# The first two value chunks of an mLSTM layer: a quarter of the contraction in seven products instead of eight

## The chip, the cores and the metric

The kernel runs on one core of one Trainium2 chip. The time is device microseconds of one execution; the figure before is the median of three runs, 1020.14 us (1020.08 to 1020.18). One more execution was taken with the hardware profiler; all durations, starts and shares below are of that one.

Engines by their names in the profile: PE is TensorE (PEld its weight loads), DVE VectorE, ACT ScalarE, POOL GpSimd, SP SyncE.

## The reference, cut to what matters

A decoder trunk of two layers, model width 2048, 256 tokens, fp32. The second layer is an xLSTM mLSTM with 8 heads (width of keys 128, of values 256):

```python
u = hn @ o_w_in[j]
qk = u[..., 0:2 * C_QK]                       # 2048 columns: queries and keys
v = u[..., 2 * C_QK:2 * C_QK + C_WIDTH]       # 2048 columns: the values, four chunks of 512
...                                           # output gate, silu gate, input and forget gates
qk = jax.nn.silu(causal_conv(qk, c_conv_w[j], c_conv_b[j]))
yc = mlstm(q, k, v, li, lf)                   # needs q, k, v and the gates
yc = head_rmsnorm(yc, c_norm[j]) * jax.nn.sigmoid(og) * jax.nn.silu(z)
h = h + yc @ o_w_out[j]
```

## The kernel before

**Products.** Every projection is computed with the activations (128 contraction rows x 128 tokens) held in TensorE and 512 columns of weights streamed, into a 128x512 PSUM bank for each half of the tokens. A number is kept as a high and a low part, and one product of two such numbers is three matmuls: high by high, high by low, low by high. A chunk of 512 columns has a contraction of 2048: four quarters, each 4 x 128 rows, two halves of the tokens, three matmuls, so 24 matmuls a quarter and 96 a chunk (`quarter_tok`, L211 to L213; `product`, L235, where three lines are one).

**Weights.** They come from HBM as 128x1024 tiles of 512 KB, two to a quarter, issued by SyncE into a ring of five (`raw`). ScalarE casts a tile to its high part (`whi`, L137 or L221) and VectorE subtracts that to get the low part (`wlo`, L138 or L222), into rings of four. A tile can be cast only once TensorE has read the tile four places ahead of it.

**Seven products (`seven`).** For two chunks of columns at once, one quarter of the contraction (`kq` = 0) can be done as a 2x2 matrix product in seven instead of eight, by the well-known scheme of Strassen and Winograd: two halves of the tokens, two halves of the quarter, two chunks. Each of the products is six matmuls. It needs four sums of activations (`combos`, made beforehand, here for the quarter 0 by `early()`, kept in `qs`), and sums of weights: the tile X (first chunk, first half) becomes W = X + the second chunk's first half, then W + Y, then that plus Z; the tile Y becomes Y + the second chunk's first half. Sums of two loaded tiles are additions on VectorE (`add`, L310), or, with `acc`, a transfer issued by POOL that adds while it writes (`add_loaded`, L314), which can start once the tile has been split for its own use. The results lie in four banks A, F, B and E; ScalarE copies A into F and its negative into B (L345, L346), saves B twice to SBUF (`keep`, L322), and VectorE adds what is left with `soon` (L318). The other three quarters are plain (`plain`). The order of the pieces is the string `a5a6.2aA7b.4F.bb` (L26): a digit is a product, a and b are the plain quarters of the first and second chunk, a point is a pump, A and F hand out a bank.

**Order of the work.** Side work is written as generators, called lanes. `pump()` makes one step of every lane, behind the latest product, cast, split and load; it is called in each quarter after the first half of the tokens, and at the points. `drain(lane)` runs a lane to its end. A scheduler then orders each engine's instructions by priorities, and `high_priority` lifts weight splits (400) and the copies at the end of a chunk (450). An engine executes its own list in order; where an instruction waits, what stands behind it waits as well.

**Around the change.** The four chunks of queries and keys come first (`oqk`); each is written to HBM and read back transposed by POOL (`features`, L686 and L689), then goes through the causal convolution as three VectorE operations of some 254 columns for each of 16 pieces (L1218) and a multiplication (L1222). Then the four value chunks (`ov`). In them run the lanes of the features, of the gates (`gate_stats`, L1257 to L1285: 8x256 rows of scans and sums; it ends in `split_rows`, L424 to L426, which makes the tile s8 of the running maxima) and of the heads: `mix(c)` takes a pair of heads, called head c below (0 to 3). Its steps are the spread of a row of s8 over all partitions by TensorE (L431), decays on VectorE and ScalarE (L1305 to L1311), high and low parts of queries and keys (L1322, L1323), scores (L1329 to L1331), their high and low parts (L1334, L1335), and the sums over values (L1349). Values go from their bank to SBUF with a row factor (L1394, L1395). When the two halves of chunk 0 are out, `values` drains two feature lanes and starts the four heads' lanes.

Chunks 2 and 3 of the values are made by `seven`; chunks 0 and 1 by `project_tok`.

Of the kernel before, what the change touches and what calls it, by code (L numbers as in the profile page):

```python
# [11 lines left out]
F32 = mybir.dt.float32  # L12
# [7 lines left out]
P = 128  # L20
# [25 lines left out]
def trunk(ctx: ExitStack, tc: tile.TileContext, a, out):  # L46
# [22 lines left out]
    def step(lane):  # L69
        q = lanes.get(lane)  # L70
        while q:
            if next(q[0], lanes) is not lanes:
                return True
            q.pop(0)
        return False
# [8 lines left out]
    def drain(*which):  # L84
        for lane in which:
            while step(lane):
                pass
# [75 lines left out]
    def project_tok(w, j, act, before=None, begun=None):  # L163

        ps = begun or [pm.tile([P, 512], F32, name="mm", tag="mm") for _ in range(2)]
        for kq in range(1 if begun else 0, 4):
            if before is not None:
                before(kq)
            quarter_tok(w, j, kq, act, ps)
        return ps  # L170
# [16 lines left out]
    def two_and_seven(w, act, before, where, places, home=None, begin=None):  # L187

        qs = {}
        start("combos", combos(act, 0, qs, *where))  # L190
        for c, ps in enumerate(project_two(w, act, before)):
            for hf in range(2):
                yield c, hf, ps[hf]
        drain("combos")
        if begin is not None:
            begin()
        for b, hf, src in seven(w, 2, act, qs, (0,), *places(), home and home()):
            yield 2 + b, hf, src

    def quarter_tok(w, j, kq, act, ps):  # L200

        parts = load_weights(w[4 * j + kq])
        for hf in range(2):
            for kk in range(4):
                k = kq * 4 + kk
                hi, lo = parts[kk // 2]
                c = (kk % 2) * 512
                ah, al, _ = act[k // 2]
                xh, xl = (tokens(x, k % 2, hf) for x in (ah, al))
                wh, wl = hi[:, c:c + 512], lo[:, c:c + 512]  # L210
                te.matmul(ps[hf], xh, wh, start=(k == 0), stop=False, skip_group_check=True)  # L211
                te.matmul(ps[hf], xh, wl, start=False, stop=False, skip_group_check=True)  # L212
                last["pe"] = te.matmul(ps[hf], xl, wh, start=False, stop=(k == KT - 1), skip_group_check=True).ins  # L213
            if hf == 0:
                pump()
# [374 lines left out]
    def ready(act, lane):  # L590

        def before(kq):
            while 2 * kq + 1 not in act:
                step(f"{lane}{kq}")
        return before
# [14 lines left out]
    def ple_gate(hq, parts, pls, rp, hss, gain, lane, more):  # L610

        nxt = {}
        for c, hf, src in parts:
            drain("pg")
            th = tp.tile([P, 512], F32, name="th", tag="th")
            h = hq[c][:, hf]
            s.activation(th, src, AF.Tanh, scale=0.5)
            v.scalar_tensor_tensor(th, th, 1.0, pls[c][hf], op0=ALU.add, op1=ALU.mult)
            v.scalar_tensor_tensor(h, th, rp[:, hf:hf + 1], h, op0=ALU.mult, op1=ALU.add)
            if not hf:  # L620
                continue
            start(f"{lane}{c}", to_features(hq[c], c, nxt, gain, lane, more))
            step(f"{lane}{c}")
            for hf in range(2):
                squared(hq[c][:, hf], hss[:, c, hf:hf + 1])
        return nxt
# [14 lines left out]
    acth = []  # L641
# [133 lines left out]
    if True:  # L775
        ew = a["ew"]
        fs, qs, ks, xcs = {}, {}, {}, {}
# [313 lines left out]
        for g in range(2):  # L1091
            ps = project_tok(ew, 6 + g, acth)
# [33 lines left out]
    def pieces(tile):  # L1126
        return iter([tile[:, 0:512], tile[:, 512:1024]]).__next__
# [30 lines left out]
    acth = ple_gate(hq, two_and_seven(a["g0"], act, ready(act, "fe"), (e0, "q4", 2), in_e0), pls, rp0, hss0, "on", "fg", gate_sums)  # L1158
# [34 lines left out]
    with tc.tile_pool(name="m1", bufs=2) as m1:  # L1193
# [32 lines left out]
        qs = {}  # L1226
# [148 lines left out]
        turn = []  # L1375

        def value_halves():
            for j in range(2):
                for hf, ps in enumerate(project_tok(a["ov"], j, acth)):
                    yield j, hf, ps  # L1380
            drain("combos", "spill")
            store_of.extend(hp.tile([P, 1024], F32, name="pr", tag="h") for _ in range(2))
            for b, hf, src in seven(a["ov"], 2, acth, qs, (0,), chain, part, acc=True):
                yield 2 + b, hf, src

        def values():
            for j, hf, src in value_halves():
                if hf == 0:
                    vt = m1.tile([P, 2, 2, VW], F32R, name="vt", tag="vt", bufs=6)
                    gp.memset(vt.bitcast(F32)[:, :, :, 256:VW], 1.0)  # L1390
                    vl = ap.tile([P, 1024], F32R, name="vl", tag="ahl").rearrange("p (h i e) -> p h i e", h=2, i=2)
                with tc.high_priority(offset=450):
                    src = src.rearrange("p (i e) -> p i e", i=2)
                    s.activation(vt[:, hf, :, 0:256], src, AF.Copy, scale=norm["rt"][:, hf:hf + 1])  # L1394
                    v.scalar_tensor_tensor(vl[:, hf], src, norm["rt"][:, hf:hf + 1], vt[:, hf, :, 0:256].bitcast(F32),  # L1395
                                           op0=ALU.mult, op1=ALU.subtract)
                if hf == 0:
                    continue
                vts.append((vt, vl))
                if j == 0:  # L1400
                    drain("qk0", "qk2")
                    for c in range(4):
                        start("mix", mix(c))
                    start("mix", mix_norm())
# [36 lines left out]
        for jj in (0, 2):  # L1441
            us = [m1.tile([P, 2, 512], F32, name="u", tag="vt", bufs=6) for _ in range(2)]
            for b, hf, src in pair(a["oz"], jj, True):
                j, u = jj + b, us[b]
# [292 lines left out]
```

## Time and profile before

| | |
|---|---|
| median of three runs | 1020.14 us |
| the profiled execution | 1020.23 us |
| its span, first to last instruction | 1018.4 us |
| granted TensorE clock | 0.998 |
| TensorE busy | 1009.4 us, 99% |
| VectorE busy | 842.8 us, 83% |
| ScalarE busy | 661.4 us, 65% |
| POOL busy | 101.3 us, 10% |
| first product of value chunk 0 | starts at 561.38 us of the span |

Matmuls overlap in their pipe: a matmul's row lasts from its start to its modelled end, so a list of starts tells the pace, and the busy time of a group counts the overlap. Rows of the chain of waits end where the next begins. In a view by windows, the number in brackets behind a busy time is the count of instructions. Instructions of the same line and shape that follow each other are joined in one row, with their count behind an x.

### The profile page before, as it was taken

The numbers are of one execution on the slowest core, as the hardware profiler recorded it, in microseconds if no ns is written. First come the engines' busy times: TensorE is split into PE (matmuls) and PEld (weight loads), VectorE is DVE, ScalarE is ACT, GpSimd is POOL, SyncE is SP. The second block draws the span as 40 slices with busy tenths as digits, with TensorE's granted clock in tenths as the row PEclk, the third lists the DMA queues.
The fourth block names the chain that finished last, engine by engine and source line by source line (L and its number), as shares of the span: only waits on it lengthen the run. The fifth ranks groups of instructions, "written<-read, shape, count | busy, mean of one in ns | idle before, by whom it ended". The sixth has DMA issues, their size and how long they took to land.

```text
span 1018.4 us, 14515 instructions
## 1 busy us (share of the span) xinstructions
PE 1009.4 (99%) x5158; PEld 838.1 (82%) x5158; DVE 842.8 (83%) x1234; ACT 661.4 (65%) x949; POOL 101.3 (10%) x182
## 2 busy tenths in 40 slices
PE   9999999999999999999999999999999999999996
PEld 8888888888888888888888888888888888888886
DVE  7858969969687887898669997888889997999794
ACT  7675554686875554666557877776676777466562
POOL 0111101011111112021011100000011110102000
PEclk9999999999999999999999999999999999999999
DMA  9987756567778799487798757567879889696852
GB/s 364 330 233 240 225 177 197 166 204 225 251 235 305 238 315 291 155 284 249 258 337 250 228 166 227 166 208 201 256 193 283 233 249 356 181 288 217 279 186 83
DMA packets 69816, 242.66 MB, mean 238 GB/s; under 512 B 9040, under 2 KB 10448, under 8 KB 69744
## 3 DMA queue, kind: packets, MB, share of 16 engines
q1 hardware_dynamic: 56016, 198.08, 58.7%
q0 software_dynamic: 13296, 43.13, 16.1%
q8 instruction: 40, 0.66, 0.3%
q10 hardware_dynamic: 432, 0.52, 0.1%
q14 instruction: 32, 0.26, 0.1%
HBM read 221.78 MB, written 19.92 MB: 237 GB/s over the span
## 4 chain that ended last, share of the span: by engine, by line
PE 99%; ACT 0%; DMA 0%; issue 0%; DVE 0%; ACTq 0%; POOLq 0%
PE mm L235 29%; PE mm L211 14%; PE mm L212 14%; PE mm L213 14%; PE mx L235 8%; PE mx L211 3%; PE mx L212 3%; PE mx L213 3%; PE mm L517 1%; PE nu L1349 1%; PE mx L517 1%; PE mm L1562 1%; PE mm L1561 1%; PE mm L1563 1%; PE st L213 1%; PE st L235 1%
## 5 line engine op out<-in xcount | busy, mean ns | idle before, releaser
L137 ACT CAST whi<-raw 128x1024 fp32r<-128x1024 f32 (+1 forms) x309 | 322.6, 1047 | 211.3 <-PE mm L213 95.2
L138 DVE TENSOR_TENSOR wlo<-raw,whi 128x1024 fp32r<-128x1024 f32 (+1 forms) x309 | 371.6, 1213 | 104.0 <-ACT whi L137 97.8
L211 PE MATMUL mm<-whi,ahl 128*128 128x512 f32 x640 | 250.5, 392 | 0.0
L212 PE MATMUL mm<-wlo,ahl 128*128 128x512 f32 x640 | 249.4, 390 | 0.0
L213 PE MATMUL mm<-whi,ahl 128*128 128x512 f32 x640 | 249.3, 389 | 0.0
L235 PE MATMUL mm<-whi,ahl 128*128 128x512 f32 x720 | 231.8, 390 | 0.0
L235 PEld LDWEIGHTS mm<-whi,ahl 128*128 128x128 f32 x720 | 135.2, 188 | 27.9
L211 PEld LDWEIGHTS mm<-whi,ahl 128*128 128x128 f32 x640 | 120.2, 188 | 25.5 <-issue 0.4
L213 PEld LDWEIGHTS mm<-whi,ahl 128*128 128x128 f32 x640 | 120.2, 188 | 25.1
L235 PE MATMUL mm<-wlo,ahl 128*128 128x512 f32 x360 | 140.5, 390 | 0.0
L212 PEld LDWEIGHTS mm<-wlo,ahl 128*128 128x128 f32 x640 | 120.2, 188 | 24.3
L222 DVE TENSOR_TENSOR wlo<-ch,whi 128x1024 fp32r<-128x1024 f32 x67 | 81.1, 1221 | 12.5 <-ACT whi L221 11.1
L221 ACT CAST whi<-ch 128x1024 fp32r<-128x1024 f32 x67 | 70.1, 1050 | 26.8 <-PE mm L235 13.8
L235 PEld LDWEIGHTS mm<-wlo,ahl 128*128 128x128 f32 x360 | 67.6, 188 | 14.1 <-DVE wlo L222 0.3
L235 PE MATMUL mx<-whi,ahl 128*128 128x512 f32 x192 | 63.3, 390 | 0.0
L212 PE MATMUL mx<-wlo,ahl 128*128 128x512 f32 x128 | 49.8, 389 | 0.0
L213 PE MATMUL mx<-whi,ahl 128*128 128x512 f32 x128 | 49.8, 389 | 0.0
L211 PE MATMUL mx<-whi,ahl 128*128 128x512 f32 x128 | 49.8, 389 | 0.0
L235 PE MATMUL mm<-whi,q 128*128 128x512 f32 x144 | 49.1, 391 | 0.0
L235 PEld LDWEIGHTS mx<-whi,ahl 128*128 128x128 f32 x192 | 36.1, 188 | 7.9 <-ACT xr L575 0.4
L235 PE MATMUL mx<-wlo,ahl 128*128 128x512 f32 x96 | 37.4, 390 | 0.0
L235 PEld LDWEIGHTS mm<-whi,q 128*128 128x128 f32 x144 | 27.0, 188 | 5.7
(389 smaller groups left out, 1318.5 us busy)
## 6 DMA issues: line engine op xcount, KB each, us to landing
raw<-in_ew_dram SPq DMA_DIRECT2D x64, 512.0 KB, 5.2
raw<-in_g_dram SPq DMA_DIRECT2D x60, 512.0 KB, 4.5
raw<-in_oqk_dram SPq DMA_DIRECT2D x32, 512.0 KB, 5.5
raw<-in_eo_dram SPq DMA_DIRECT2D x30, 512.0 KB, 5.1
raw<-in_oo_dram SPq DMA_DIRECT2D x30, 512.0 KB, 6.4
raw<-in_ov_dram SPq DMA_DIRECT2D x29, 512.0 KB, 4.2
raw<-in_oog_dram SPq DMA_DIRECT2D x24, 512.0 KB, 4.1
raw<-in_oz_dram SPq DMA_DIRECT2D x20, 512.0 KB, 5.1
```

The source lines that it names most:

```text
L137: last["act"] = s.copy(h, r).ins
L138: last["dve"] = v.tensor_tensor(out=l, in0=r, in1=h.bitcast(F32), op=ALU.subtract).ins
L211: te.matmul(ps[hf], xh, wh, start=(k == 0), stop=False, skip_group_check=True)
L212: te.matmul(ps[hf], xh, wl, start=False, stop=False, skip_group_check=True)
L213: last["pe"] = te.matmul(ps[hf], xl, wh, start=False, stop=(k == KT - 1), skip_group_check=True).ins
L221: last["act"] = s.copy(hi, r).ins
L222: last["dve"] = v.tensor_tensor(out=lo, in0=r, in1=hi.bitcast(F32), op=ALU.subtract).ins
L235: last["pe"] = te.matmul(o, x, y, start=(first and k + i == 0), stop=(end and k == n - 1 and i == 2), skip_group_check=True).ins
L517: last["pe"] = te.matmul(ps[hf][:, o:o + w_], tokens(pact[x], k, hf), (hi, lo)[y][:, k * 512 + o:k * 512 + o + w_], start=(n == mine[0]), ...
L1349: te.matmul(ps[:, 0:n], x[:, i, o:o + P], y[:, b, i], start=(b == 0 and x is sh and y is vh), stop=(b == hf and y is vl))
L1561: te.matmul(o, xh, wh, start=(k == 0), stop=False)
L1562: te.matmul(o, xh, wl, start=False, stop=False)
```

## The change

Chunks 0 and 1 of the values are made by `seven` as chunks 2 and 3 are, with the first quarter of the contraction in seven products and two of the sums of weights by accumulating transfers (`acc=True`). The saved banks lie in a tile of the pool `m1` with the tag "vt". The lane of the sums of activations (`combos`) is drained ahead of this, and the lane `spill` behind the first two chunks, as before.

```diff
         def value_halves():
-            for j in range(2):
-                for hf, ps in enumerate(project_tok(a["ov"], j, acth)):
-                    yield j, hf, ps
-            drain("combos", "spill")
+            drain("combos")
+            pr = pieces(m1.tile([P, 1024], F32, name="pr", tag="vt", bufs=6))
+            yield from seven(a["ov"], 0, acth, qs, (0,), chain, pr, acc=True)
+            drain("spill")
             store_of.extend(hp.tile([P, 1024], F32, name="pr", tag="h") for _ in range(2))
             for b, hf, src in seven(a["ov"], 2, acth, qs, (0,), chain, part, acc=True):
                 yield 2 + b, hf, src
```

The order of the chunks' halves changes with it: both chunks are ready close together, at the end of 186 matmuls, where chunk 0 was ready after 96 and chunk 1 after 192. The heads' lanes start after chunk 0's second half, as they did.

TensorE's list where the first spread of a head stands, before (mm_5562 is a bank of value chunk 1, s8 the split maxima):

```order
L211 MATMUL mm_5562<-whi_5571,ahl_4392 128x512
L212 MATMUL mm_5562<-wlo_5572,ahl_4392 128x512
L213 MATMUL mm_5562<-whi_5571,ahl_4392 128x512
L431 MATMUL mx_5588<-s8_5445,identr_229 128x256 x2
L211 MATMUL mm_5563<-whi_5565,ahl_4386 128x512
L212 MATMUL mm_5563<-wlo_5566,ahl_4386 128x512
```

And with the change (mm_5351 is the bank B of the first seven products, mm_5779 the bank A of the second):

```order
L235 MATMUL mm_5351<-whi_5727,ahl_4810 128x512
L235 MATMUL mm_5351<-whi_5733,ahl_4816 128x512
L431 MATMUL mx_5680<-s8_5488,identr_229 128x256 x2
L235 MATMUL mm_5351<-wlo_5734,ahl_4816 128x512
L235 MATMUL mm_5351<-whi_5733,ahl_4816 128x512 x2
L235 MATMUL mm_5351<-wlo_5734,ahl_4816 128x512
L235 MATMUL mm_5351<-whi_5733,ahl_4816 128x512
L235 MATMUL mm_5779<-whi_5784,ahl_4386 128x512
```

The spread stood in the first quarter of chunk 1, behind 108 matmuls of the values; now it stands behind 181, five matmuls ahead of the end of both chunks.

VectorE's list ahead of the row L426 that completes s8, before:

```order
L425 CAST s8_5445<-Mx_5341 8x256
L1222 SCALAR_TENSOR_TENSOR qk_5414<-th_5496,qk_5414 128x512
L138 TENSOR_TENSOR wlo_5572<-raw_5570,whi_5571 128x1024
L1395 SCALAR_TENSOR_TENSOR vl_5557<-mm_5347,rcr_4629,vt_5555 128x512
L426 TENSOR_TENSOR s8_5445<-Mx_5341,s8_5445 8x256
L138 TENSOR_TENSOR wlo_5612<-raw_5610,whi_5611 128x1024
```

And with the change (ch_5782 and ch_5797 are the tiles X and Y of the second seven products, pr_5347 the saved bank of the first):

```order
L138 TENSOR_TENSOR wlo_5734<-raw_5732,whi_5733 128x1024
L1276 TENSOR_TENSOR ae_5342<-li_5337,Bc_5340 8x256
L1395 SCALAR_TENSOR_TENSOR vl_5588<-pr_5347,rcr_4629,vt_5586 128x512
L1278 TENSOR_TENSOR ae_5342<-Bc_5340,Mx_5341 8x256
L318 TENSOR_TENSOR pr_5347<-mx_5348,pr_5347 128x512
L425 CAST s8_5488<-Mx_5341 8x256
L1285 STREAM_TRANSPOSE aT_5343<-ae_5342 32x64
L426 TENSOR_TENSOR s8_5488<-Mx_5341,s8_5488 8x256
```

L426 stood behind a split of chunk 1's first quarter; now all weight splits of both chunks stand ahead of it, and the first two of chunks 2 and 3.

TensorE's list at the first scores, before (wlo_5719 and wlo_5725 belong to the last quarter of chunk 1):

```order
L213 MATMUL mm_5562<-whi_5724,ahl_4816 128x512
L1329 MATMUL mx_5741<-qhl_5699,khl_5700 128x256 x3
L1330 MATMUL mx_5741<-qk_5147,qk_5414 128x128
L1329 MATMUL mx_5747<-qhl_5699,khl_5700 128x256 x3
L1330 MATMUL mx_5747<-qk_5147,qk_5414 128x128
L211 MATMUL mm_5563<-whi_5718,ahl_4810 128x512
```

And with the change (mm_5779 and mm_5780 are banks of the second seven products):

```order
L1329 MATMUL mx_5833<-qhl_5750,khl_5751 128x256 x2
L235 MATMUL mm_5779<-wlo_5997,ahl_4816 128x512
L235 MATMUL mm_5779<-whi_5996,ahl_4816 128x512
L235 MATMUL mm_5780<-whi_5990,ahl_4810 128x512
L235 MATMUL mm_5780<-wlo_5991,ahl_4810 128x512
L1329 MATMUL mx_5833<-qhl_5750,khl_5751 128x256
L1330 MATMUL mx_5833<-qk_5147,qk_5457 128x128
```

The scores stood in one piece in chunk 1; now they stand in pieces in the second seven products.

## The prediction

> **What bounds the kernel now.** I read the page's busy shares and its chain first, then TensorE's waits.
>
> ```profile
> span 1018.4 us, 14515 instructions
> PE 1009.4 (99%) x5158; PEld 838.1 (82%) x5158; DVE 842.8 (83%) x1234; ACT 661.4 (65%) x949; POOL 101.3 (10%) x182
> PE 99%; ACT 0%; DMA 0%; issue 0%; DVE 0%; ACTq 0%; POOLq 0%
> PE st L99 <- PEq L1728: 0.8, 1, 0.8
> ```
>
> The chain that ended last is TensorE from end to end, and in the whole run it waits once, 0.8 us at the start. So the time is the number of matmuls by their pitch, and two things alone can move it: fewer products, or a first wait. The pitch comes from the list of starts and from the chain:
>
> ```profile
> 572.34 0.39 PE L211 MATMUL mm<-whi,ahl 128*128 128x512 f32 x1
> 572.57 0.39 PE L212 MATMUL mm<-wlo,ahl 128*128 128x512 f32 x1
> ...
> 672.09 14.77 PE mm L235 x65
> ```
>
> Starts lie 0.23 us apart, and 14.77/65 = 0.227 us, for the matmuls of the plain chunks and of the seven products alike (0.2266 used below). The 0.39 us of a row is its latency in the pipe. The windows show who could make TensorE wait (the change lies from 561 to 647):
>
> ```profile
> core 0: us, PE busy (x) PEld busy (x) DVE busy (x) ACT busy (x) POOL busy (x), PEclk, DMA share, GB/s
> 540.00:560.00 20.00, 20.00 (x90) 16.57 (x89) 20.00 (x34) 15.39 (x26) 2.92 (x7) 1.00 0.81 256
> 560.00:580.00 20.00, 20.00 (x91) 16.53 (x90) 18.63 (x34) 16.31 (x24) 2.75 (x5) 1.00 0.80 241
> 580.00:600.00 20.00, 20.00 (x90) 16.57 (x90) 19.66 (x37) 15.14 (x25) 0.00 (x0) 1.00 0.57 184
> 600.00:620.00 20.00, 20.00 (x103) 16.99 (x103) 16.66 (x24) 15.96 (x31) 2.01 (x4) 1.00 0.64 162
> 620.00:640.00 20.00, 20.00 (x105) 17.13 (x103) 15.71 (x23) 15.36 (x32) 0.00 (x0) 1.00 0.68 232
> 640.00:660.00 20.00, 20.00 (x107) 16.93 (x106) 15.87 (x24) 13.30 (x27) 0.00 (x0) 1.00 0.48 152
> ```
>
> VectorE is busy 58.3 of 60 us (97%) from 540 to 600, where the first two value chunks are made, and 79 to 83% in each stretch behind that. ScalarE is at 65 to 82%. TensorE's clock is full. A change that takes work from TensorE and gives it to VectorE just there is where a wait can arise.
>
> **What it removes.** The first quarter of the contraction for two chunks and two token halves is 8 products of six matmuls, and 7 now. So 6 x 0.2266 = **1.36 us** less on TensorE, 0.13% of the run. By the mean of a row it would be another sum:
>
> ```profile
> L235 PE MATMUL mm<-whi,ahl 128*128 128x512 f32 x720 | 231.8, 390 | 0.0
> ```
>
> 6 x 0.390 = 2.34 us. The Trainium skill speaks against that second sum ("Trainium Kernel Development and Optimization", Performance Expectations: a matmul's busy time is a bad metric, since matmuls are pipelined, the weight loads' busy share a good one). By that rule the trace agrees: 16.57 us of weight loads in 20 us for about 89 matmuls, and 20/89 = 0.225 us for one.
>
> **What it adds on VectorE.** Three more weight splits (L222 and L138 together, seven weight tiles for four in that quarter), two sums of weights (L310), three combinations of banks (L318). Their durations and pitches:
>
> ```profile
> L222 DVE TENSOR_TENSOR wlo<-ch,whi 128x1024 fp32r<-128x1024 f32 x67 | 81.1, 1221 | 12.5 <-ACT whi L221 11.1
> L310 DVE TENSOR_TENSOR ch<-ch,raw 128x1024 f32<-128x1024 f32 x17 | 20.4, 1217 | 0.1
> L318 DVE TENSOR_TENSOR pr<-mm,pr 128x512 f32<-128x512 f32 x18 | 12.3, 681 | 0.2 <-PE mm L235 0.2
> ...
> 590.08 1.22 DVE L138 TENSOR_TENSOR wlo<-raw,whi 128x1024 fp32r<-128x1024 f32 x1
> 591.22 0.87 DVE L1218 SCALAR_TENSOR_TENSOR qk<-xr,prm,qk 128x254 f32<-128x254 f32 x2
> 592.01 1.22 DVE L138 TENSOR_TENSOR wlo<-raw,whi 128x1024 fp32r<-128x1024 f32 x1
> 593.14 0.68 DVE L1323 TENSOR_TENSOR qhl<-qk,qhl 128x512 fp32r<-128x512 f32 x1
> 593.74 2.06 DVE L1218 SCALAR_TENSOR_TENSOR qk<-xr,prm,qk 128x253 f32<-128x253 f32 x5
> ```
>
> A row lasts longer than its place: from start to start a 128x1024 takes 1.14 us (590.08 to 591.22), one convolution step L1218 0.40 (591.22 to 592.01 for two), a 512-wide one 0.60 (593.14 to 593.74). The addition is 5 x 1.14 + 3 x 0.60 = **7.5 us** of VectorE inside a stretch that had 1.7 us of idle time in 60. The Trainium skill would make it a little more ("VectorE: DVE Perf Modes", The DRAIN you can't avoid: the next operation waits until the pipe is empty, unless it isn't held): 5 x 1.22 + 3 x 0.68 = 8.1 us. The starts above, nearer than the durations, don't bear that out.
>
> **What hides the rest.** ScalarE gets three more casts, a copy and a negation of a bank, and two bank copies, some 5 us; it idles 3.7 to 4.9 us of each 20, over two stretches, so its total fits. Casts there already wait for a ring slot that TensorE frees:
>
> ```profile
> 560.05 1.05 ACT L137 CAST whi<-raw 128x1024 fp32r<-128x1024 f32 x1 [0.67 <-PE mm L213]
> ```
>
> SyncE issues 15 half-blocks instead of 16, and POOL two accumulating transfers. The kernel has such transfers in its second seven products:
>
> ```profile
> 601.42 0.93 POOL L314 DMA_DIRECT2D ch<-in_ov_dram  x1 [29.02 <-DVE wlo L222]
> DMA to landing us min/median/max: 5.6/6.6/7.6
> ...
> 556.06 1.23 DVE L138 TENSOR_TENSOR wlo<-raw,whi 128x1024 fp32r<-128x1024 f32 x1
> ```
>
> The first can be issued once X is split: the first value split starts at 556.06 now and X's stands in its place, so about 557.6. It lands 5.6 to 7.6 us later, at 563.2 to 565.2; a cast (1.05) and a split (1.14) make it usable by 567.4 at the latest. TensorE needs it after A, E and one plain quarter: 36 products from 561.38, so at 569.54. Hidden, with 2.1 us to spare; without that cover the cost would be all that it is late. The second has a whole plain quarter more. Behind it on POOL stand the four copies into the features' scratch (L689), which wait for their own transfer until about 570.2 anyway: no cost. Below nothing none of these can go, since TensorE waits for none of them now.
>
> **What is moved, and where it waits.** In the new order the first row spread of the mixing heads (L431, in TensorE's own order) stands after 181 of the 186 products of the two chunks, not after 108 of 192, and the gate rows before it on VectorE (the statistics L1268 to L426) are spread among the splits. TensorE can't pass it. The rows of before for the pieces:
>
> ```profile
> 561.38 0.23 PE mm L211
> 569.54 0.24 PE mx L1264 x2
> 586.10 0.23 PE mx L431 x2
> ...
> 570.25 0.40 DVE L1268 TENSOR_TENSOR li<-mx,hrs 8x256 f32<-8x256 f32 x1
> 582.19 0.75 DVE L1395 SCALAR_TENSOR_TENSOR vl<-mm,rcr,vt 128x512 fp32r<-128x512 f32 x1
> 582.97 0.41 DVE L426 TENSOR_TENSOR s<-Mx,s 8x256 fp32r<-8x256 f32 x1
> ```
>
> Value products begin at 561.38 (T). Before, L426 ended at 583.38 and L431 started at 586.10: 2.7 us of slack. Now the two ledgers:
>
> *TensorE* reaches L431 at T + 181 x 0.2266 + 0.24 (L1264) = T+41.25.
>
> *VectorE*: the low half of the second tile of the second plain quarter can't be made before its ring slot is free. That slot's last reader is the 30th product, T+6.8; with the cast, T+7.9. From that split to L426 there are, in the new order, 53 operations: 16 of 128x1024 (18.2 us), 16 L1218 (6.4), 5 of 512 columns (3.0), 2 L1395 (0.66 by start to start, 1.3), and 14 small ones on rows or memsets (5.3, from the starts between L1268 and L426 above: 0.2 to 0.7 each). Sum 34.2, so L426 ends at T+42.15: **0.9 us late**.
>
> What is late next, in the same way: from there to the split keys that the scores L1329 read are 34 operations on VectorE (13 x 1.14, 8 x 0.40, 3 x 0.60, 2 x 0.66, 7 transposes of 0.25, 0.34), 23.2 us, against 97 products and 0.48 us of scores on TensorE, 22.45: **0.75 more**. Last, the heads stand closer. From a head's spread L431 to its first sum L1349 lay 25.9 us for head 0 (586.10 to 612.03) and 16.3 for head 1 (614.40 to 630.73):
>
> ```profile
> 612.03 2.14 PE nu L1349 x18
> 614.40 0.40 PE mx L431 x2
> 630.73 2.14 PE nu L1349 x18
> 632.88 0.23 PE mx L431 x2
> 652.99 0.41 PE mx L431 x2
> ```
>
> In the new order head 1 has 25 products there, 5.7 us, and its chain of decay, exponentials, scores and splits over three engines adds up to about 6.2 by rows of these kinds: **0.5 late**. Sum of the waits 2.15 us; each may be off by 0.6 or so, since a ledger of 53 operations at 0.02 us each is uncertain by 1 us. Bounds: nothing (VectorE keeps up, no wait), and all 7.5 us of new VectorE work standing in front of TensorE. I take 2.15, nearer to nothing, since VectorE idles 4 us of each 20 from 600 on.
>
> Net: -1.36 + 2.15 = +0.8. The profiled execution took 1020.23 us and the median 1020.14, 0.09 less; so 1021.0 for a profiled run, **1020.9** for the median.
>
> **The rivals.** All in terms of 1020.14; what this kernel's runs can tell from no change I set at 0.2%, 2.04 us.
>
> *A: VectorE keeps up* and the gain stands: 1020.14 - 1.36 = 1018.8. For it: chunks 2 and 3 are made by the same seven products from 604 on, without a wait of TensorE. Against it: there VectorE is 79 to 83% busy, here 97%. Chance 0.25.
>
> *B: the forecast*, three waits eat the gain: 1020.9. Chance 0.55.
>
> *C: the other side.* The late VectorE is late for everything behind it: one mechanism, splits that tie with TensorE. The tightest, the second tile of chunk 1's second plain quarter, ends by the ledger just as its product comes up, and the four heads' spreads stand 32, 13 and 10 us apart by the new order, instead of 28, 18 and 20, each with such a chain behind it. If VectorE's delay is 1 us more than I count, each of the wait places pays it, some 4 us in all: 1020.14 - 1.36 + 4 = 1022.8. It decides once the first wait is over 1.5 us. Chance 0.18.
>
> *D: the accumulating transfer holds the first seven products.* It needs a landing over 9.8 us, against the 7.6 that the trace shows; a wait of 1 us would give 1019.8. Chance 0.02, in which the time is within 0.2%.
>
> **How the numbers follow.** Range 1018.7 (A, full gain) to 1023.2 (C and a little more); what is left out above is the bound of 7.5 us (1026.3). Faster by over 0.2% (under 1018.1) needs more than the whole gain: 0.03. Slower by over 0.2% (over 1022.2): C and the upper tail of B, 0.19. The rest, 0.78, within. My likeliest case's own range is 1019.6 to 1022.0.
>
> **What would show it.** Right: TensorE's waits list L431 behind the split of the maxima (about 0.9 us), L1329 behind the keys, L1349 behind a head's split; TensorE's products 6 fewer; VectorE 100% busy from 569 to 604. Wrong: no new row among the waits (then A), a wait of L235 for a split (C), or one for a transfer (D). If VectorE shows idle time before L426, the ledger is wrong in its anchor and not in its sum.

## The result, and the profile after

The changed kernel takes **1028.26 us** (median of 6, 1027.31 to 1028.51) against 1020.16 us of the kernel before on the same chip: ratio 1.0078, 95% interval 1.0065 to 1.0091. It is 8 us slower. The forecast was 1020.9, with a range to 1023.2.

Its page, for the execution that was profiled (1028.51 us): span, busy shares, and the shares of the chain that ended last.

```profile
span 1026.7 us, 14530 instructions
PE 1011.9 (99%) x5152; PEld 838.6 (82%) x5152; DVE 850.5 (83%) x1242; ACT 665.8 (65%) x956; POOL 103.5 (10%) x184
PE 89%; DVE 7%; issue 1%; ACT 1%; DMA 1%; ACTq 0%; DVEq 0%; POOLq 0%
```

TensorE has its 6 matmuls fewer (5152 for 5158), VectorE its 8 operations and 7.7 us more (forecast 7.5). But the chain, all TensorE before, now runs over VectorE for 7% of the span (ahead of a wait it follows VectorE's list back, so this share is not the time lost). TensorE's waits, which were one of 0.8 us at the start:

```profile
PE nu L1349 <- ACT sh L1334: 4.4, 1, 4.4
PE mx L431 <- DVE s L426: 0.8, 1, 0.8
...
PE mx L1329 <- ACT khl L1322: 0.2, 1, 0.2
PE mx L1329 <- DVE khl L1323: 0.2, 1, 0.2
```

The waits at L431 and at L1329 are the two that the forecast worked out. The one of 4.4 us is not: it is head 2's first sum over values. In windows of 20 us (columns as before: busy time of TensorE, its weight loads, VectorE, ScalarE, POOL, then clock, share of the DMA engines, GB/s):

```profile
580.00:600.00 20.00, 20.00 (x89) 16.40 (x88) 19.94 (x32) 17.64 (x26) 0.00 (x0) 1.00 0.70 236
600.00:620.00 20.00, 19.19 (x86) 15.58 (x85) 19.70 (x32) 11.87 (x16) 1.90 (x3) 1.00 0.62 163
620.00:640.00 20.00, 19.53 (x100) 15.58 (x99) 17.52 (x29) 15.54 (x32) 0.11 (x1) 1.00 0.67 222
640.00:660.00 20.00, 19.44 (x100) 15.72 (x98) 17.12 (x25) 14.64 (x34) 0.00 (x0) 1.00 0.38 132
660.00:680.00 20.00, 16.20 (x76) 14.38 (x77) 13.48 (x20) 13.62 (x29) 0.00 (x0) 0.83 0.51 173
```

VectorE is 98 to 100% busy from 580 to 620, where it had been at 83% from 600 on. In the last row TensorE idles 3.8 us and its clock is 0.83. None of the other engines is full there: VectorE works 13.5 of 20 us. So the big loss stands in a stretch with room on every engine. The chain of waits through it, in order of time:

```profile
655.58 3.88 PE mm L235 x17
659.46 0.02 issue
659.48 0.57 ACT mm L345
660.05 0.97 ACT whi L221
661.02 0.02 issue
661.04 1.22 DVE wlo L222
662.27 0.48 DVE wt L1331
...
662.82 0.84 ACT sh L1334
663.66 0.14 issue
663.80 4.27 PE nu L1349 x18
```

The last six of the 17 matmuls fill bank A of the *next* stage's seven products, the output gate's. ScalarE copies that bank (L345) and then casts a tile W of that stage (L221); VectorE splits it (L222); only then comes the second half of head 2's scores (L1331), whose matmuls had been done by 655.58, then their high part (L1334), and TensorE, which has nothing else ahead in its list, goes on. VectorE's list at that place tells why (wt_6123 and mx_6161, mx_6167 are head 2; raw_6344, ch_6318, ch_6332 are the output gate's weights):

```
L1331 SCALAR_TENSOR_TENSOR wt_6123<-mx_6161,wt_6123 128x384
L310 TENSOR_TENSOR ch_6318<-ch_6318,ch_6332 128x1024
L138 TENSOR_TENSOR wlo_6350<-raw_6348,whi_6349 128x1024
L138 TENSOR_TENSOR wlo_6356<-raw_6354,whi_6355 128x1024
L222 TENSOR_TENSOR wlo_6401<-raw_6344,whi_6400 128x1024
L1331 SCALAR_TENSOR_TENSOR wt_6123<-mx_6167,wt_6123 128x384
```

Four weight operations of the next stage stand between the two halves of one head, and the last of them hangs on TensorE itself, by way of ScalarE. In the kernel before one L318 stood there, with no copy of a bank ahead of it. VectorE's own rows show which of the two counts:

```profile
657.36 1.21 DVE L310 TENSOR_TENSOR ch<-ch 128x1024 f32<-128x1024 f32 x1
658.49 2.35 DVE L138 TENSOR_TENSOR wlo<-raw,whi 128x1024 fp32r<-128x1024 f32 x2
661.04 1.22 DVE L222 TENSOR_TENSOR wlo<-raw,whi 128x1024 fp32r<-128x1024 f32 x1 [0.21 <-ACT whi L221]
```

VectorE stood idle for 0.21 us between the two L1331. The rest of the delay, 4.6 us at 1.14 each, is the four operations themselves: the chain of waits names L345 and L221 because they ended last, but head 2 would have been nearly as late had L222 not waited for them.

Behind the wait TensorE is slow. In windows of 2 us, TensorE alone (busy time, granted clock, share of the DMA engines, GB/s):

```profile
660.00:662.00 2.00, 0.00 (x0) 1.00 0.61 209
662.00:664.00 2.00, 0.20 (x1) 0.52 0.87 270
664.00:666.00 2.00, 2.00 (x10) 0.50 0.80 307
666.00:668.00 2.00, 2.00 (x11) 0.50 0.02 8
668.00:670.00 2.00, 2.00 (x10) 0.77 0.00 0
670.00:672.00 2.00, 2.00 (x10) 1.00 0.00 0
```

The clock is at a half from about 662.1 to 668.9. Head 2's 18 sums took 4.27 us; head 0's and head 1's took 2.14 us each before.

**The account**, from the starts in TensorE's list from 561 to 690, each start against the start ahead of it and the usual pitch. A wait costs 0.16 us more than its idle time, which counts from the end of a 0.39 us row:

| term | forecast | measured |
|---|---|---|
| six matmuls fewer | -1.36 | -1.36 |
| wait at L431 | 0.9 | 0.97 |
| waits at L1329 | 0.75 | 0.79 |
| head 1's sums | 0.5 | 0 |
| head 2's sums | none | 4.51 |
| half clock behind that | none | 2.3 |
| scores in more pieces | none | 0.55 |
| not placed (rest of the +8.04 below) | none | 0.3 |
| sum | +0.8 | +8.04 |

The term on the scores: the four heads' scores take 5.21 us of TensorE, waits taken out, where they took 4.66, because the change's list cuts them into eight pieces where they stood in five. No run isolates it.

To compare profiled executions I take the time from the start of the first matmul of the first projection to the first L517 at about 830 us in the chain of waits, well behind the change: 810.60 us before (16.49 to 827.09), 818.64 after, **+8.04**. Behind that point all runs take 191.3 to 191.5 us. Ahead of it lies the start of the program, where the first projection begins at 15.9 to 18.5 us in one execution or the other (a wait of L517 for L486 belongs to it); that scatter is in the medians. "Stretch" below is this difference to 810.60.

### The profile page after: what moved, and what is told of

It is laid out like the page before. It is cut to its first block, busy times and chain, and to the rows that moved or that the text cites. A ratio compares the mean times of both kernels' runs of the same rounds, so it can differ in the third digit from the quotient of the medians.

```text
span 1026.7 us, 14530 instructions
## 1 busy us (share of the span) xinstructions
PE 1011.9 (99%) x5152; PEld 838.6 (82%) x5152; DVE 850.5 (83%) x1242; ACT 665.8 (65%) x956; POOL 103.5 (10%) x184
## 4 chain that ended last, share of the span: by engine, by line
PE 89%; DVE 7%; issue 1%; ACT 1%; DMA 1%; ACTq 0%; DVEq 0%; POOLq 0%
PE mm L235 27%; PE mm L211 12%; PE mm L213 12%; PE mm L212 12%; PE mx L235 8%; PE mx L213 3%; PE mx L212 3%; PE mx L211 3%; DVE wlo L138 2%; DVE qk L1218 2%; DVE wlo L222 1%; PE mm L517 1%; PE nu L1349 1%; PE mx L517 1%; PE mm L1562 1%
## 5 line engine op out<-in xcount | busy, mean ns | idle before, releaser
L138 DVE TENSOR_TENSOR wlo<-raw,whi 128x1024 fp32r<-128x1024 f32 (+1 forms) x305 | 366.1, 1211 | 101.8 <-ACT whi L137 96.2
L137 ACT CAST whi<-raw 128x1024 fp32r<-128x1024 f32 (+1 forms) x305 | 318.0, 1046 | 202.5 <-PE mm L213 84.4
L235 PE MATMUL mm<-whi,ahl 128*128 128x512 f32 x804 | 258.4, 390 | 0.0
L211 PE MATMUL mm<-whi,ahl 128*128 128x512 f32 x576 | 225.3, 392 | 0.0
L212 PE MATMUL mm<-wlo,ahl 128*128 128x512 f32 x576 | 224.2, 389 | 0.0
L213 PE MATMUL mm<-whi,ahl 128*128 128x512 f32 x576 | 224.1, 389 | 0.0
L235 PEld LDWEIGHTS mm<-whi,ahl 128*128 128x128 f32 x804 | 150.7, 188 | 31.1
L235 PE MATMUL mm<-wlo,ahl 128*128 128x512 f32 x402 | 156.7, 390 | 0.0
L211 PEld LDWEIGHTS mm<-whi,ahl 128*128 128x128 f32 x576 | 108.1, 188 | 23.0 <-issue 0.4
L213 PEld LDWEIGHTS mm<-whi,ahl 128*128 128x128 f32 x576 | 108.1, 188 | 22.5
L222 DVE TENSOR_TENSOR wlo<-ch,whi 128x1024 fp32r<-128x1024 f32 x73 | 88.2, 1219 | 11.3 <-ACT whi L221 9.6
L221 ACT CAST whi<-ch 128x1024 fp32r<-128x1024 f32 x73 | 76.2, 1049 | 26.4 <-PE mm L235 13.9
L235 PEld LDWEIGHTS mm<-wlo,ahl 128*128 128x128 f32 x402 | 75.5, 188 | 15.5
L235 PE MATMUL mx<-whi,ahl 128*128 128x512 f32 x216 | 71.3, 390 | 0.0
L235 PE MATMUL mm<-whi,q 128*128 128x512 f32 x156 | 53.1, 390 | 0.0
L211 PE MATMUL mx<-whi,ahl 128*128 128x512 f32 x128 | 49.8, 389 | 0.0
L212 PE MATMUL mx<-wlo,ahl 128*128 128x512 f32 x128 | 49.8, 389 | 0.0
L213 PE MATMUL mx<-whi,ahl 128*128 128x512 f32 x128 | 49.8, 389 | 0.0
L235 PEld LDWEIGHTS mx<-whi,ahl 128*128 128x128 f32 x216 | 40.5, 188 | 8.7 <-issue 0.4
L235 PE MATMUL mx<-wlo,ahl 128*128 128x512 f32 x108 | 42.2, 391 | 0.0
L235 PEld LDWEIGHTS mm<-whi,q 128*128 128x128 f32 x156 | 29.3, 188 | 6.2
```

The lines of the kernel that those rows point to most:

```text
L137: last["act"] = s.copy(h, r).ins
L138: last["dve"] = v.tensor_tensor(out=l, in0=r, in1=h.bitcast(F32), op=ALU.subtract).ins
L221: last["act"] = s.copy(hi, r).ins
L222: last["dve"] = v.tensor_tensor(out=lo, in0=r, in1=hi.bitcast(F32), op=ALU.subtract).ins
L235: last["pe"] = te.matmul(o, x, y, start=(first and k + i == 0), stop=(end and k == n - 1 and i == 2), skip_group_check=True).ins
```

## The experiments

**Theory Q**: the loss is a matter of place in the queues, head 2's work behind operations of the next stage, and the half clock follows from the length of that wait. **Rival V**: VectorE has 7.5 us too much to do, and the wait will turn up somewhere whatever is moved. **Rival S**: four heads that start late are in each other's way.

### One line lifted

```diff
-                v.scalar_tensor_tensor(wt[:, i, :], sc[:, 0:384], SC, ...)
+                with tc.high_priority(offset=450 if j == 2 else 0):
+                    v.scalar_tensor_tensor(wt[:, i, :], sc[:, 0:384], SC, ...)
```

> The changed kernel with one line lifted: head 2's two products of scores and decay (L1331) get the priority that weight splits and bank copies have, so on VectorE no sum or split of the next stage's weights stands between them. Theory Q (order in the queues: head 2's sums waited behind a split of the output gate's weights, whose cast stood on ScalarE behind a bank copy that waited for TensorE): the wait of 4.5 us at head 2's first L1349 and the 2.4 us at half clock behind it go, the small waits at L431 and L1329 (1.0 and 0.8 from start to start) stay: 1028.3 - 6.9 = 1021.4, between 1020.8 and 1022.2, granted clock 1.00 in every stretch. Rival V (VectorE has simply too much to do, 7.5 us more): the time moves to another wait, 1026 to 1029.

Measured: 1028.25 us, ratio 1.0080 (1.0065 to 1.0095), stretch +8.4. Nothing gained. Head 2's first sums now start at 657.5 without a wait (in TensorE's list they moved up too, from behind 17 matmuls to behind 9); the wait is one step on. TensorE's longest wait in this run, and then its chain of waits there:

```profile
PE mx L235 <- ACT sq L1355: 3.6, 1, 3.6
```

```profile
662.09 0.35 ACT mm L345
...
662.47 1.08 ACT whi L221
...
663.58 0.05 DVE wlo L222
...
664.72 0.16 DVE den L1353
...
665.19 0.20 ACT sq L1355
...
665.43 2.93 PE mx L235 x6
```

Bank E of the output gate's seven products is one of three that the heads' sums use too. It is free once head 2's sums are read out, and those readings (L1353, L1355) stood behind L345, L221 and L222. The forecast of this run failed, and the time fell where V had put it. The common part of both waits is L345, L221, L222, and again VectorE was hardly idle (0.05 us ahead of L222): what stood in front was work of its own. Q had to be widened from one row to all of head 2's tail.

### The gate rows first; both; the late start alone

The gate rows L1264 to L426 in a block with `tc.high_priority(offset=450)`:

> The changed kernel with the gate rows (L1264 to L426) lifted to the priority of the bank copies, so that the first spread L431 stands 9.7 us earlier in TensorE's list and its operand is made early. The heads keep their later start. By its order no weight split stands between head 2's two L1331. Theory Q: no wait at L431 (-1.0) and none of 4.5 us at head 2, no half clock: 1019.2 to 1021.0. Rival V: the gate rows done early push weight splits back, TensorE waits for those: 1023 or more, with waits of L235 for a split.

Measured: 1023.66 us, 1.0034 (1.0024 to 1.0045), stretch +1.84. In the profiled execution the 4.5 us wait, the half clock and the wait at L431 are gone, without a change to head 2's own priority: moving the first spread moved the heads, and head 2's two L1331 stood next to each other. But by the time this is V's forecast (1023 or more) and not Q's (up to 1021.0), and so is this run's longest wait behind 560:

```profile
PE mx L235 <- DVE wlo L138: 1.9, 1, 1.9
```

At 588 a split is late, because the gate rows went ahead of it. The median is 3.65 us above that of the kernel before, twice the stretch. The later start of the profiled execution (17.44 for 16.49) has 0.95 of it; the rest isn't in its trace. Four of the eight executions, with a mean clock of 0.996 for the 0.998 of the profiled one, took 1023.4 to 1024.3 us, so a piece of half clock in those is likely, but no trace of them was kept.

> Both lifts together, the gate rows and head 2's L1331. Theory Q: as with the gate rows alone, 1019.2 to 1020.5; if all waits go, 1020.1 - 1.36 = 1018.8. Rival V: 1023 or more.

Measured: 1023.18 us, 1.0032 (1.0019 to 1.0045), stretch +1.76: V's range once more (Q had said up to 1020.5). The lift of head 2's line adds nothing here, since it had nothing left to remove.

For the late start alone, the kernel before with one character changed:

```diff
-                if j == 0:
+                if j == 1:
                     drain("qk0", "qk2")
                     for c in range(4):
                         start("mix", mix(c))
```

> The kernel before, chunks 0 and 1 plain, with one part of what the change does: the lanes of the four heads start only when chunk 1 is out (192 products) instead of chunk 0 (96). By its order no split stands between a head's two L1331. Theory Q (it is the place in the queues that costs, not the late start): within 1 us of the kernel before, 1019.8 to 1021.5. Rival S (four heads pressed into less room are late for each other): 1024 or more, without any seven products in the first chunks.

Measured: 1020.13 us, 1.0003 (0.9994 to 1.0012), stretch -0.26, no wait of TensorE in the whole stretch. Heads that start 96 matmuls later cost nothing by themselves. Their spreads stand 25, 15 and 20 us apart in this run; whether heads still closer to each other cost something is answered by the run with all tails lifted, below.

### The whole tail lifted

L1331, L1334, L1335, L1352, L1353 and L1355 with `tc.high_priority(offset=450)`, for head 2 and then for all heads:

> The run with head 2's L1331 alone lifted lost as much as the changed kernel, one step on: head 2's sums were in time, and the next seven products' bank E then waited 3.65 us for the reading out of head 2's sums (L1353 on VectorE, L1355 on ScalarE), which stood behind the same bank copy L345, cast L221 and split L222. Here all of head 2's tail is lifted: L1331, L1334, L1335, L1352, L1353 and L1355. Theory Q, mended (whatever of head 2 stands behind the copy of bank A of the output gate's seven products comes too late, since TensorE has nothing else to do): no wait over 1 us is left there, clock 1.00, the waits of 1.0 and 0.8 us at L431 and L1329 stay: 1020.8 to 1022.0. Rival V (too much work, whatever the order): a wait of 3 us or more turns up at the next step again, 1026 to 1029.

Measured: 1022.40 us, 1.0024 (1.0015 to 1.0033), stretch +3.09; no wait over 0.8 us is left and the clock is 1.00 from 560 to 700. The time is 0.4 us above what Q allowed: small waits of L235 for L345 and L346 came instead (0.56 and 0.34 idle).

> The same lift for the tails of all four heads. By the order head 2 is then through before bank A of the next seven products begins. Theory Q: as before, 1020.8 to 1022.0, with the wait at E gone altogether. Rival V: lifted heads push weight splits back and TensorE waits for these, 1023 or more.

Measured: 1021.73 us, 1.0014 (1.0004 to 1.0023), stretch +1.21: within Q's range. All of TensorE's waits behind 560:

```profile
PE mx L431 <- DVE s L426: 0.8, 1, 0.8
...
PE mx L1329 <- ACT khl L1322: 0.3, 1, 0.3
PE mx L1329 <- DVE khl L1323: 0.2, 1, 0.2
```

This is the state that the prediction had described: the two small waits, 1.82 us from start to start here. Less the 1.36 that makes +0.46 for the +1.21 measured; the scores in pieces have 0.42 of the difference (5.08 us for 4.66), the rest is not placed. So the place of the heads' tails in the lists was worth 6.8 us of the stretch. S falls here too: the spreads start at 603.8, 635.7, 646.3 and 656.2, the last three 10 us apart and closer than in the changed kernel, and no head waits for its sums.

### Without the heads

> The changed kernel with the four heads left out (their sums replaced by constants; everything ahead of them, the convolutions and gate rows among it, is still made). Some 13.5 us of TensorE go with them. Theory Q (the seven products themselves cost nothing but what they save; the loss lies in the heads' passage): 1.4 us below the kernel before without heads, about 1005.2, no wait over 0.3 us in the first two value chunks. Rival V (the 7.5 us of VectorE are too much by themselves): weight splits late in the first seven products, no gain or a loss of 1 us or more against the kernel before without heads.

> The kernel before with the four heads left out in the same way: the base for the run of the changed kernel without heads. Both theories: about 1006.6, no waits of TensorE.

Measured: 1004.86 and 1005.56 us, ratios to the kernel before 0.9844 (0.9829 to 0.9859) and 0.9857 (0.9841 to 0.9873). The changed one is 0.70 us lower, half of the 1.36, and the two intervals overlap. The base is not clean either: it was forecast without waits, and its profiled execution, at 1008.05 the slowest of four, has three (0.98 us idle for a split at 585, 1.36 for L346 at 612, 0.28 for a split at 463). So the pair doesn't show how large the gain is. What speaks against V is the changed kernel's own trace: VectorE is busy 19.94 of 20 us from 580 to 600, and TensorE waits nowhere for a split, its one wait behind 560 being 0.19 us for L346: full is not late.

### The clock by itself

In the kernel before, far from the change: behind a product on bank B, n small copies on ScalarE, one reading the other, and a small matmul that reads the last and that the next product has to follow.

The code is cut to what matters (the block has a priority of 500, and `o` is a bank of its own):

```diff
                 product(B, combo(1), split(W))
+                # once, in the output gate's chunks 2 and 3
+                z = bank[:, 0:64]
+                for _ in range(n):
+                    y = tp.tile([P, 64], F32R, ...)
+                    s.copy(y, z)
+                    z = y
+                last["pe"] = te.matmul(o[0:64, 0:64], z, z, start=True, stop=True).ins
```

> The kernel before, with one wait of TensorE put in on purpose in a stage that the change doesn't touch (the output gate's chunks 2 and 3): behind the product on bank B a chain of 3 dependent small copies on ScalarE, and a small matmul that reads the last, which the next product has to follow. The gap should be some 2 to 2.6 us. Theory K (TensorE's granted clock falls to a half when it has had nothing to do for some 2.6 us, as in the changed kernel between 659.5 and 662): lost time equals the gap, clock 1.00. Rival (the half clock belongs to the mixing heads or to the load of transfers there): the same here.

> The same with 7 copies, a gap of 3.2 to 4.2 us. Theory K: clock 0.50 in the windows behind it, and some 2.4 us lost beside the gap. Rival: clock 1.00, the gap alone lost.

> The same with 12 copies, a gap of 4.5 to 6 us. Theory K: clock 0.50, 2 to 2.5 us lost beside the gap. Rival: the gap alone.

The wait that was made, by TensorE's waits of the runs with 3, 7 and 12 copies:

```profile
PE st L248 <- ACT gz L245: 2.0, 1, 2.0
```

```profile
PE st L248 <- ACT gz L245: 3.1, 1, 3.1
```

```profile
PE st L248 <- ACT gz L245: 4.5, 1, 4.5
```

The windows of 2 us in which TensorE goes on (TensorE alone, columns as above), in the same order of the runs; it starts again at 720.1, 721.5 and 722.2:

```profile
720.00:722.00 2.00, 1.86 (x9) 1.00 1.03 213
722.00:724.00 2.00, 2.00 (x11) 1.00 0.95 313
```

```profile
722.00:724.00 2.00, 2.00 (x8) 0.67 0.91 301
724.00:726.00 2.00, 2.00 (x7) 0.50 0.59 236
726.00:728.00 2.00, 2.00 (x10) 0.97 0.00 0
```

```profile
722.00:724.00 2.00, 1.83 (x5) 0.53 0.97 387
724.00:726.00 2.00, 2.00 (x7) 0.62 0.07 27
726.00:728.00 2.00, 2.00 (x10) 1.00 0.00 0
```

Stretches +2.19, +4.92 and +6.40: after the gap of 2.0 us only the gap is lost (2.18 from start to start), after 3.1 and 4.5 us some 1.7 us more (4.92 less 3.28, 6.40 less 4.66). Each is one execution. Theory K holds in the main, with 1.7 where I had expected 2.4, and the rival falls: there are no heads here, and behind the gap of 2.0 us the clock is full under the same load of transfers (213 and 313 GB/s). Its 2.6 us does not hold: the clock fell 2.6 us after TensorE's last row had ended in the changed kernel, but 4.3 and 4.5 us after it behind the gaps of 3.1 and 4.5. The stretch of half clock is about 3.4 us in both (0.67 in the first window of 2 us is 1.3 us at a half, then 2 us more). In the changed kernel it was 6.8, twice that, of which the first 1.7 us fell in the wait.

The Trainium skill has a rule for this ("TensorE: Matmul & The Clock Gate", What's actually happening, and Why this matters for your kernels): the clock is halved after an idle window of about 3.4 us and full again after a busy one; keep gaps under some 3 us. The runs agree on the advice, no half clock at 2.0, and on the steps of 3.4 us; on the idle window they differ, since a gap of 3.1 us was enough, and in the changed kernel the clock fell 2.6 us into the wait.

### A middle way for the gate rows

All tails lifted, and the gate rows by 100, below the weight splits.

> The changed kernel with the tails of all four heads lifted as before, and the gate rows L1264 to L426 lifted by 100, above the convolution steps but below the weight splits (the run with the gate rows above the splits made a split 1.9 us late at 588). By the ledger of the prediction L426 then ends at T+32.1 where TensorE asks for it at T+31.8, and the split that was late comes up at T+27, just in time. Theory Q: waits of 0.5 us there and 0.4 to 0.8 us at L1329 are left, 1020.1 - 1.36 + 1.1 = 1019.9, between 1019.2 and 1020.6. Rival V: a wait of 2 us or more at a split, 1021.5 or more.

Measured: 1021.56 us, 1.0015 (1.0006 to 1.0024), stretch +1.16, against +1.21 without the gate rows' lift. Q's range was missed, and V's (1021.5 or more) is met by 0.06 us, without its wait of 2 us at a split. The wait at L431 is gone, but a split at 588 (0.36 idle) and L235 behind the copy L345 at 607 (0.62) came for it. What one row gains another gives back.

### VectorE's volume

With all tails lifted, the keys' convolution left out in part: `for k in range(2, -1 if j < 2 else 2, -1)` at L1216.

> The run with the tails of all four heads lifted, with part of VectorE's other work left out: of the convolution of the keys (the third and fourth chunk of queries and keys) the three VectorE steps of each piece, 24 operations of 0.40 us, 9.6 us, more than the 7.5 us that the change adds. Theory L (the small waits at L431, 1.0, and L1329, 0.8, are VectorE's volume between 569 and 627): both gone, 1.8 us less than with the tails lifted alone, 1021.7 - 1.8 = 1019.9, between 1019.2 and 1020.5. Rival (they are due to the order in which rows stand, not to the volume): waits of 1.5 us or more stay, 1021.2 or more.

Measured: 1019.68 us, 0.9994 (0.9981 to 1.0007), stretch -0.82. The waits at L431 and L1329 are gone; what is left in the value stage is one of 0.21:

```profile
PE mm L235 <- ACT mm L345: 0.2, 1, 0.2
```

So with 9.6 us less on VectorE the small waits go, as Theory L had it, and 0.82 of the 1.36 us is there. That it is the volume and not the order isn't shown by this run alone: the lists moved with it. The first spread stands behind 138 matmuls of the values, not 181, and starts at 592.5 instead of 603.8, and each head's scores stand in one piece again (4.66 us). As a time the gain is within what can be told from no change.

### Chunk 0 first

All tails lifted, the order string of the first seven products "a5a6.2aA4F.7b.bb". In this run chunk 0's second half is handed out before product 7 is in it, so its values lack that term; the work is the same.

> The run with all tails lifted and the first seven products in another order, so that chunk 0 is complete after 108 products (96 before the change) and the heads' lanes start there. By TensorE's list head 0's sums then stand 0.4 us of work behind its scores. Theory Q (a wait is the length of the chain over the other engines less the work that stands between): from the scores over L1331, 0.5 twice, L1334, 0.84, and the hand-overs the chain is some 2.0 to 2.6 us, so a wait of 1.6 to 2.2 us at head 0's L1349, under the length at which the clock falls, and the waits for the keys ahead of it as before: 1021.0 to 1023.5. Rival (an earlier start is what the heads lacked): no wait over 1 us, 1018.8 to 1020.

Measured: 1036.27 us, 1.0143 (1.0128 to 1.0158), stretch +15.7. Both forecasts missed by far. TensorE's waits of this run, and the window from 600 to 620 (columns as in the first windows above):

```profile
PE mx L1329 <- ACT khl L1322: 8.5, 1, 8.5
PE mm L235 <- DVE pr L318: 1.7, 1, 1.7
PE nu L1349 <- issue: 1.6, 1, 1.6
```

```profile
600.00:620.00 20.00, 10.91 (x47) 8.54 (x45) 18.05 (x35) 9.12 (x15) 1.94 (x4) 0.84 0.54 131
```

The scores asked for keys whose convolution and split were still to come on VectorE, which worked on at 90% while TensorE stood for 8.5 us. I had counted the chain behind the scores and not the one ahead of them. Where VectorE is full, an earlier place in TensorE's list meant a longer wait here. The two other waits and a stretch of half clock from 613.7 to 627.3 are in the 15.7 as well.

No version came out faster than the kernel before by more than can be measured. Whether the gain can be had with the whole convolution, by another order, stays open.

## Why the prediction was wrong

**Right.** The gain of six matmuls by their pitch: the same pitch stands in the trace after, and the run with part of the convolution left out keeps 0.82 us of it. The hidden transfers: the first accumulating one landed at 563.7, inside the 563.2 to 565.2 of the forecast, and TensorE waits for none. The ledgers: L426 was to end at T+42.15, which is 603.5, and ended at 603.65; its wait came out as 0.97 for 0.9, those at L1329 as 0.79 for 0.75. The anchor was right too: the split from which the ledger counts starts at 569.44, T+8.1 for the forecast T+7.9, and VectorE is busy 34.3 of the 35 us from 569 to 604. That fits work that stands in line; the run with less convolution agrees and doesn't isolate it. The 97% of VectorE was read from 540 on, 21 us ahead of the first value matmul; from 560 to 600 alone it is 96%, which changes nothing.

**Wrong.** The step that failed is "what is late next", in its last part: "the heads stand closer". I took the head with the least TensorE work between spread and sums (head 1, 5.7 us), set the head's own chain of 6.2 us against it, and got 0.5; that wait did not come. Head 2, with 8.0 us, was passed over as having room. What I had not read is whose operations stand *between* the parts of a head's chain on VectorE and ScalarE. There the next stage's weight operations, lifted by 400, had come ahead of head 2's: four on VectorE, 4.6 us. This wait is not a sum of durations of a head's own rows; its length, 4.35 us idle, is that of the last steps of the detour, L345, L221, L222, L1331, L1334, from the end of TensorE's last matmul on. The list of the changed kernel showed it. The sign "L1349 behind a head's split" did appear, at head 2 and not at head 1, and for this other reason: that is luck.

The second thing that the sum had no term for is the clock, 2.3 us. I read the clock as full and took it as given, though a wait of 3.1 us changes it, as the runs with copies show, and one of 2.0 does not. The third and smaller one is the scores in more pieces, 0.55.

The bounds were wrong in kind. "All 7.5 us of new VectorE work" is a bound for waits by volume; a wait by order isn't bounded by the work that was added. Rival C named the other side with the wrong mechanism, splits that tie with TensorE: no split was late by over 0.1 us in the changed kernel. Rival A did not occur: VectorE, full as the forecast read it, did not keep up. D did not occur either.

## What to carry to other kernels

When a change moves a stage against its neighbour, read the new lists of all engines for one pattern: an operation that TensorE will ask for soon, behind operations of the next stage that have a higher priority, the more so if one of those waits for TensorE itself. A mean busy share below 100% on VectorE and ScalarE did not protect against it here; lifting one row only passed the wait to the next, and the whole tail had to go ahead. Count a wait of TensorE of 3 us or more with its half clock, here 1.7 to 2.8 us more; and a saving of 0.1% in a kernel without a single wait is smaller than the price of one misplaced row.

## What the runs showed of the hardware

The granted clock fell to a half with a gap of 3.1 us without a matmul (and of 3.6, 4.4 and 4.5), not with one of 2.0. It stayed for 3.4 us or a multiple of that: 3.4 behind the gaps of 3.1 and 4.5 that were made, about 6.8 in the changed kernel, 13.6 in the run with chunk 0 first (613.7 to 627.3). From the end of TensorE's last row to the fall it took 2.6 us in the changed kernel, 4.3 and 4.5 behind the gaps that were made and 4.8 in the run with chunk 0 first, so there was no fixed delay. Beside the idle time, 1.7 us were lost to the 3.4, and 2.3 and 2.8 to the longer ones of the changed kernel and of the run with one line lifted. The half clock began while TensorE still waited (662.1 in the changed kernel, work from 663.8) or when it had begun again (about 722.7 in the run with 7 copies, work from 721.5).

The time lost to a wait of TensorE is 0.16 us longer than the idle time that the profile shows (0.97 for 0.81, 4.51 for 4.35, 2.18 for 2.02), since rows of 0.39 us that start 0.23 us apart overlap by that much when nothing waits.
